# Block sums of two seven-product projections made by accumulating transfers, and two attention heads placed between the first two products

## The chip, the cores and the metric

The kernel runs on one core of one Trainium2 chip. The metric is the time of one execution on the device in microseconds (us). A core has five engines, each with an instruction queue of its own: PE (matrix multiplication), ACT (activation functions, copies, casts), DVE (elementwise work), POOL, and SP, which here only issues transfers. POOL issues transfers too. Engines wait for one another through semaphores; in the rows of instructions further down, "waits DVE_49" is such a wait, DMAHW names the semaphores of transfers issued by SP, and DMASW those of transfers issued by POOL.

## The reference

The reference is one layer of a hybrid decoder trunk on 512 tokens of width 1024, in fp32, with a memory of 256 tokens:

```python
h = rmsnorm(x, norm_mix_g)
proj = h @ w_in                       # 1024 x 8192: three branches and their gates
conv_out = short_conv_mixer(...)      # causal depthwise convolution, 512 channels
sb_out = stick_breaking_attention(...)# 8 heads x 64
ret_out = retention(...)              # 4 heads x 128
up = einsum('bsnw,nwd->bsnd', branches, w_branch)
gates = sigmoid(gate_logits + b_gate)
merged = sum(gates * up, axis=2)
x = x + merged @ w_o                  # 1024 x 1024: the first output projection
h = rmsnorm(x, norm_xa_g)
mem_n = rmsnorm(mem, norm_mem_g)
q, k, v = h @ w_xq, *split(mem_n @ w_xkv)
o = softmax(q k^T / 16) v             # 4 heads x 256
x = x + o @ w_xo                      # 1024 x 1024: the second output projection
h = rmsnorm(x, norm_mlp_g)
x = x + square(relu(h @ w_up)) @ w_down
return rmsnorm(x, final_g)
```

## The kernel before

*Arithmetic.* Every fp32 operand of a matrix product is split into a high part, a cast to fp32r made on ACT, and a low part, the difference from it, made on DVE. A product is three matrix multiplications: high by high, high by low and low by high. For weights the split is `parts_of` (L111 the cast, L112 the subtraction); for the token side it is `split` (L260, L261).

*The weight stream.* Weights arrive in blocks of 128 x 1024 (512 KB), issued by SP (L214) into six buffers named `w_raw`. Their parts go into ten buffers named `w_part`. A list of items, `plan`, written out in program order, says which parts each item takes; `Stream.pump` makes the parts two steps ahead of the item that needs them. A scheduler then sets the order of the instructions on each engine; each engine works through its own list strictly in that order.

*Seven products instead of eight.* The projections by `w_o`, `w_xo` and `w_down` use a seven-product form of the 2 x 2 block product. On the weight side this is `Wide`: an entry takes eight blocks, named b11, b12, b22 and b21 with j = 0 and 1 each, and makes 14 parts of it in the order

```python
P1,0 P5,0 P1,1 P5,1 P6,0 P6,1 P3,0 P3,1 P2,0 P2,1 P7,0 P7,1 P4,0 P4,1
```

Each part is used by 12 matrix multiplications of 128x512 (L399). j halves the contraction: j = 0 takes the first 512 rows of the weight. P1 takes b11 as it is, P3 b22, P2 b21; for P5, P6, P4 the block b11 is overwritten, step by step, by a sum or difference with another block, and b12 once for P7 (`step`: L127 a subtraction, L130 an addition, on DVE). So in all there are eight block sums per projection of `w_o` and `w_xo`, each an instruction over 128 x 1024 elements.

On the token side `Pairs.make` forms the matching mixes (`pr_v`, `mg` or `xo_u`) on DVE and splits them into `pr` and `pr_b`. `items_w` lists the products: each is accumulated in PSUM and added to x (L405), at the place that the table `TO` gives.

*The two places.* `proj_norm` writes out a projection with the following RMSNorm, and is called for `w_o` and for `w_xo`.

Around `w_o`: the branch outputs are being multiplied by `w_branch`, gated by sigmoids (`gt`, L885) and merged into `mg` (L840, L841), from which the mixes are made; the gate's own products (`seven`, L329, with copies into `sv_s` and `sv_u`) run between the first products of `w_o`. `reload_x` loads x again from DRAM (`load_x`, L99, issued by POOL), since x is the residual. `mem_begin` then loads the gains `g_mem` (L93) and two tiles of the memory (`m_sb`, L928), also from POOL; ACT's norm of the memory reads them (L465).

Around `w_xo`: the products of `w_xv` end (`xv_h`, `xv_l`). Then each head h of four has its scores (`xa_scores`), softmax, the transposes of its probabilities (`xa_transpose`: `xpp` by PE, `xpT` the parts), and its output (`xa_out`: 12 matrix multiplications of `xpT` with `xv`, four copies into `xo_s` and `xo_u` at L1073 and L1074, and the pairs). Heads 0 and 1 feed the products with j = 0, heads 2 and 3 those with j = 1. Before, the order at the end is written out as

```python
    item(lambda: xa_out(2))
    item(lambda: xa_out(3))
    ...
    proj_norm(w_xo, "xo", g_mlp, lambda p: None, first_up)
```

so that both of the last heads stand ahead of every product of `w_xo`.

Of the kernel before, what the change touches and what calls it, by code (L numbers as in the profile page):

```python
# [15 lines left out]
P = 128  # L16
# [22 lines left out]
def trunk_kernel(ctx: ExitStack, tc: tile.TileContext, x, mem, par, rot, dqd, kdec, g_mix, g_xa, g_mem, g_mlp,  # L39
# [56 lines left out]
    def load_x():  # L96
        xs = [unit("x", (P, D), F32) for _ in range(NT)]
        for t in range(NT):
            pool.dma_start(out=xs[t], in_=x[t * P:(t + 1) * P, :])  # L99
        return xs  # L100
# [28 lines left out]
    def plus(out, a, b):  # L129
        dve.tensor_tensor(out=out, in0=a, in1=b, op=ALU.add)  # L130

# [42 lines left out]
    class Wide:  # L174
# [3 lines left out]
        def __init__(self, t, c):  # L178
            self.loads = [(t, c + i) for i in range(8)]
            at = dict(P1=0, P5=1, P6=4, P3=4, P2=6, P7=6, P4=6)  # L180
            self.need = [at[p] + (2 * j if at[p] < 4 else j) + 1 for p, j in ORDER]
            self.steps = [lambda raw, p=p, j=j: self.step(raw, p, j) for p, j in ORDER]
            self.parts = []

        def step(self, raw, p, j):
            b11, b12, b22, b21 = (raw[i] if i < len(raw) else None for i in (2 * j, 2 * j + 1, 4 + j, 6 + j))
            if p == "P5":
                minus(b11, b12, b11)
            elif p == "P6":
                plus(b11, b22, b11)  # L190
                plus(b12, b12, b22)
            elif p == "P4":
                minus(b11, b21, b11)
            return parts_of(dict(P3=b22, P2=b21, P7=b12).get(p, b11))

# [153 lines left out]
    class Pairs:  # L349
# [7 lines left out]
        def make(self, e, s, u):  # L357
# [14 lines left out]
            minus(u[:, 1, :], u[:, 1, :], u[:, 0, :])  # L372
# [4 lines left out]
    TO = dict(P1=(0, 0), P2=(0, 0), P3=(0, 1), P4=(2, 0), P5=(2, 1), P6=(0, 1), P7=(2, 1))  # L377

    def items_w(src, c, pairs, after=lambda p: None):
# [4 lines left out]
        def part(p, js, n):  # L384
            bank = dict(P2="p2", P5="p3", P3="p3").get(p, "p1")

            def fn(ws):
# [14 lines left out]
                def add(i):  # L402
                    t, h = TO[p]
                    dst = S["x"][t + i][:, h * 512:(h + 1) * 512]
                    dve.tensor_tensor(out=dst, in0=acc[bank, i], in1=dst, op=ALU.add)  # L405
# [7 lines left out]
            item(fn, (Wide, src, c, n, n + len(js)))  # L413
# [549 lines left out]
    def proj_norm(src, name, g, beside, after):  # L963
# [20 lines left out]
        items_w(src, 0, lambda k: S[name, k // 2].w[k % 2], ends)  # L984
# [106 lines left out]
    item(lambda: xa_out(2))  # L1091
    item(lambda: xa_out(3))
# [43 lines left out]
    proj_norm(w_xo, "xo", g_mlp, lambda p: None, first_up)  # L1136
# [152 lines left out]
```

## Time and profile before

| | us |
|---|---|
| median of 3 runs | 1032.84 |
| lowest, highest | 1031.75, 1033.41 |
| the profiled execution, its own time | 1034.26 |
| span of the profiled execution | 1032.5 |
| PE busy | 1000.0 (97%) |
| DVE busy | 732.8 (71%) |
| ACT busy | 529.3 (51%) |
| POOL busy | 69.2 (7%) |

The mean granted TensorE clock of the profiled execution is 0.992 of full speed. The span reaches from the first to the last instruction on the core; the time of an execution is a little longer. In rows of the timeline the columns are start, duration, engine, line, operation, output and input tiles with their shapes, a count, and in brackets the idle time of that engine ahead of the row and what ended it. In rows of groups the two numbers behind the bar are the busy time and the mean duration in ns, and behind the second bar the idle time ahead. A time between the start of a row and the start of the next one on the same engine is what it costs there; the durations of neighbouring rows overlap a little. In the table of windows each engine has its busy time, then the granted clock, the share of DMA engines that were busy, and GB/s. In rows of transfers the last number is the median time from issue to landing.

### The profile page before, as it was taken

To read this page: it belongs to the slowest core of one execution; us is meant where nothing else is said; L and a number is where in the kernel's file an instruction comes from. 1 tells how busy PE (TensorE), PEld (TensorE's weight loads), DVE (VectorE), ACT (ScalarE), POOL (GpSimd) and SP (SyncE) were. 2 spreads that over 40 slices of the span, in tenths; PEclk is the share of its full clock that TensorE was granted. 3 is DMA by queue.
4 is the path that set the end of the run, shared out by engine and by line. 5 is a ranking of instruction groups with operands and counts; after the bars stand their busy time and mean duration, and the time that the engine had idled before them with its cause. 6 is when DMAs were issued, how large, how long until landed. Compare 5 with 4: busy or idle time off the path is not lost.

```text
span 1032.5 us, 13357 instructions
## 1 busy us (share of the span) xinstructions
PE 1000.0 (97%) x5060; PEld 846.0 (82%) x5060; DVE 732.8 (71%) x1092; ACT 529.3 (51%) x935; POOL 69.2 (7%) x128
## 2 busy tenths in 40 slices
PE   5999999999999999998999998999999999999996
PEld 4788888888888889997798886779888888888885
DVE  5567767866453797789796469694785695686785
ACT  5475566766532245465474346464553653553543
POOL 1111103321010000001000000000000000000000
PEclk9999999999999999999899999999999999999999
DMA  8322232213222212325445210152125115215212
GB/s 326 103 82 85 83 123 99 83 42 110 74 80 84 82 46 98 103 88 186 153 174 185 92 62 21 60 189 79 41 102 177 49 62 175 91 41 184 82 42 82
DMA packets 29873, 106.28 MB, mean 103 GB/s; under 512 B 3568, under 2 KB 3568, under 8 KB 29808
## 3 DMA queue, kind: packets, MB, share of 16 engines
q1 hardware_dynamic: 27216, 98.05, 27.4%
q0 software_dynamic: 1440, 5.24, 1.4%
q10 hardware_dynamic: 1152, 2.12, 0.6%
q8 instruction: 40, 0.66, 0.3%
q14 instruction: 25, 0.20, 0.1%
HBM read 103.31 MB, written 2.10 MB: 102 GB/s over the span
## 4 chain that ended last, share of the span: by engine, by line
PE 92%; DVE 4%; DMA 1%; ACT 1%; issue 1%; SPq 0%; POOL 0%; DVEq 0%; POOLq 0%; ACTq 0%
PE p L399 21%; PE mm L272 20%; PE mm L273 20%; PE mm L271 20%; PE p L329 5%; DVE w_part L112 1%; PE o L657 1%; PE at L496 1%; PE aT L623 1%; DMA w_raw<-in_w_in_dram 1%; PE z L599 1%; PE z L600 0%; DVE w_raw L130 0%; PE ro L804 0%; PE sc L778 0%
## 5 line engine op out<-in xcount | busy, mean ns | idle before, releaser
L112 DVE TENSOR_TENSOR w_part<-w_raw,w_part 128x1024 fp32r<-128x1024 f32 (+1 forms) x228 | 274.7, 1207 | 155.1 <-ACT w_part L111 141.3
L111 ACT CAST w_part<-w_raw 128x1024 fp32r<-128x1024 f32 (+1 forms) x228 | 236.6, 1040 | 284.4 <-PE mm L272 146.0
L272 PE MATMUL mm<-hT_l,w_part 128*128 128x512 f32 (+1 forms) x704 | 268.0, 381 | 1.7 <-DVE hT_l L261 1.7
L273 PE MATMUL mm<-hT_h,w_part 128*128 128x512 f32 (+1 forms) x704 | 267.9, 381 | 0.0
L271 PE MATMUL mm<-hT_h,w_part 128*128 128x512 f32 (+1 forms) x704 | 267.3, 382 | 0.0
L399 PE MATMUL p<-w_part,pr 128*128 128x512 f32 x864 | 206.2, 394 | 3.8 <-ACT pr L260 2.7
L399 PEld LDWEIGHTS p<-w_part,pr 128*128 128x128 f32 x864 | 162.7, 190 | 40.3 <-ACT pr L260 3.1
L272 PEld LDWEIGHTS mm<-hT_l,w_part 128*128 128x128 f32 x704 | 132.5, 188 | 25.8 <-DVE hT_l L261 1.9
L273 PEld LDWEIGHTS mm<-hT_h,w_part 128*128 128x128 f32 x704 | 132.5, 188 | 24.8
L271 PEld LDWEIGHTS mm<-hT_h,w_part 128*128 128x128 f32 x704 | 131.8, 188 | 23.7
L405 DVE TENSOR_TENSOR x<-p,x 128x512 f32<-128x512 f32 x84 | 56.8, 684 | 20.5 <-PE p L399 20.4
L399 PE MATMUL p<-w_part,pr_b 128*128 128x512 f32 x144 | 37.1, 411 | 2.4 <-ACT w_part L111 2.4
L127 DVE TENSOR_TENSOR w_raw<-w_raw 128x1024 f32<-128x1024 f32 (+1 forms) x36 | 37.5, 1042 | 0.8 <-DMA w_raw<-in_w_xo_dram 0.3
L611 DVE TENSOR_TENSOR_SCAN sb_suf<-ones,sb_e 128x128 f32<-128x128 f32 (+3 forms) x32 | 29.6, 926 | 11.3 <-POOL sb_e L590 9.6
L130 DVE TENSOR_TENSOR w_raw<-w_raw 128x1024 f32<-128x1024 f32 (+1 forms) x36 | 37.4, 1039 | 0.1
L329 PE MATMUL p<-mix_h,w_part 128*128 128x256 f32 x192 | 37.0, 283 | 0.0
L399 PEld LDWEIGHTS p<-w_part,pr_b 128*128 128x128 f32 x144 | 28.5, 199 | 9.5 <-ACT w_part L111 2.8
L329 PEld LDWEIGHTS p<-mix_h,w_part 128*128 128x128 f32 x192 | 30.9, 191 | 0.2
L465 ACT ACTIVATE xn<-x 128x512 f32<-128x512 f32 x32 | 20.0, 628 | 19.4 <-DVE x L405 16.2
L614 ACT ACTIVATE sb_suf<-sb_suf 128x128 f32<-128x128 f32 (+3 forms) x32 | 15.1, 471 | 27.7 <-DVE sb_suf L613 27.7
L329 PE MATMUL p<-hT_h,w_part 128*128 128x256 f32 x144 | 28.6, 283 | 0.4 <-ACT w_part L111 0.4
L329 PE MATMUL p<-mix_l,w_part 128*128 128x256 f32 x96 | 27.1, 283 | 0.0
(225 smaller groups left out, 1466.4 us busy)
## 6 DMA issues: line engine op xcount, KB each, us to landing
w_raw<-in_w_in_dram SPq DMA_DIRECT2D x52, 512.0 KB, 3.5
w_raw<-in_w_up_dram SPq DMA_DIRECT2D x32, 512.0 KB, 3.5
w_raw<-in_w_down_dram SPq DMA_DIRECT2D x32, 512.0 KB, 3.5
w_raw<-in_w_br_dram SPq DMA_DIRECT2D x12, 512.0 KB, 3.4
w_raw<-in_w_gate_dram SPq DMA_DIRECT2D x12, 512.0 KB, 3.5
w_raw<-in_w_o_dram SPq DMA_DIRECT2D x8, 512.0 KB, 4.0
w_raw<-in_w_xk_dram SPq DMA_DIRECT2D x8, 512.0 KB, 3.5
w_raw<-in_w_xv_dram SPq DMA_DIRECT2D x8, 512.0 KB, 3.5
```

What stands on the lines that cost most here:

```text
L111: act.copy(out=wh, in_=src)
L112: dve.tensor_tensor(out=wl, in0=src, in1=wh.bitcast(F32), op=ALU.subtract)
L127: dve.tensor_tensor(out=out, in0=a, in1=b, op=ALU.subtract)
L130: dve.tensor_tensor(out=out, in0=a, in1=b, op=ALU.add)
L271: te.matmul(ps, lh, rh, start=first, stop=False)
L272: te.matmul(ps, lh, rl, start=False, stop=False)
L273: te.matmul(ps, ll, rh, start=False, stop=last)
L329: te.matmul(ps[:, :256], x[:, k, :], y, start=first and k == 0 and i == 0, stop=k == 3 and i == 2, skip_group_check=True)
L399: te.matmul(acc[bank, i], x, y, start=p in ("P1", "P5", "P2") and j + k + m == 0, stop=j == 1 and k == 1 and m == 2, skip_group_check=True)
L405: dve.tensor_tensor(out=dst, in0=acc[bank, i], in1=dst, op=ALU.add)
L465: act.activation(out=dst[:, cs], in_=src[:, cs], func=AF.Square, accum_out=ss[:, i:i + 1])
L611: dve.tensor_tensor_scan(out=suf[:, :s][:, ::-1], data0=ones[:, :s], data1=e1[:, :s][:, ::-1], initial=0.0, op0=ALU.mult, op1=ALU.add)
```

## The change

- `Summed`, a new kind of `Wide`, is used by both calls of `proj_norm`. The eight block sums of a projection are no longer instructions of DVE. They are transfers that POOL issues (L212 in the new file) with the option to add: they read the other block from DRAM once more and add it to what stands in the `w_raw` buffer. In the step of P1: b11 += b12 and b12 += b22; in that of P5: b11 += b22; in that of P6: b11 += b21. Each is issued after the parts of that step have been made, which read the buffer.
- Since an accumulating transfer only adds, the signs are changed throughout: `Wide.step` adds where it subtracted, `Pairs.make` forms its mixes with the opposite sign (`neg`, a scalar_tensor_tensor in place of a tensor_tensor), and `TO` says for each product whether it is added to x or subtracted from it. `Wide` itself stays in use for `w_down`, with its sums on DVE.
- `load_x` is issued by SP instead of POOL.
- `last_heads` puts heads 2 and 3 between the first product (P1,0) and the second (P5,0) of `w_xo`.

```diff
     def load_x():
...
-            pool.dma_start(out=xs[t], in_=x[t * P:(t + 1) * P, :])
+            nc.sync.dma_start(out=xs[t], in_=x[t * P:(t + 1) * P, :])
...
     class Wide:
...
             if p == "P5":
-                minus(b11, b12, b11)
+                plus(b11, b11, b12)
             elif p == "P6":
-                plus(b11, b22, b11)
+                plus(b11, b11, b22)
                 plus(b12, b12, b22)
             elif p == "P4":
-                minus(b11, b21, b11)
+                plus(b11, b11, b21)
             return parts_of(dict(P3=b22, P2=b21, P7=b12).get(p, b11))
+
+    class Summed(Wide):
+        def __init__(self, t, c):
+            super().__init__(t, c)
+            self.need = [n + (n in (1, 3)) for n in self.need]
+
+        def step(self, raw, p, j):
+            b11, b12, b22, b21 = (raw[i] if i < len(raw) else None for i in (2 * j, 2 * j + 1, 4 + j, 6 + j))
+
+            def acc(dst, i):
+                pool.dma_start(out=dst, in_=self.t[self.c + i], accum_op=ALU.add)
+
+            parts = parts_of(dict(P3=b22, P2=b21, P7=b12).get(p, b11))
+            if p == "P1":
+                acc(b11, 2 * j + 1)
+                acc(b12, 4 + j)
+            elif p in ("P5", "P6"):
+                acc(b11, 4 + j if p == "P5" else 6 + j)
+            return parts
...
+            def neg(out, a, b):
+                dve.scalar_tensor_tensor(out=out, in0=a, scalar=-1.0, in1=b, op0=ALU.mult, op1=ALU.subtract)
...
-            minus(v, u[:, 0:1, :].broadcast_to([P, 2, 256]), s)
+            minus(v, s, u[:, 0:1, :].broadcast_to([P, 2, 256]))
             put(("A11", "A22"), s)
-            minus(u[:, 0, :], s[:, 0, :], v[:, 1, :])
+            neg(u[:, 0, :], s[:, 0, :], v[:, 1, :])
...
-            minus(u[:, 1, :], u[:, 1, :], u[:, 0, :])
+            neg(u[:, 1, :], u[:, 1, :], u[:, 0, :])
...
-    TO = dict(P1=(0, 0), P2=(0, 0), P3=(0, 1), P4=(2, 0), P5=(2, 1), P6=(0, 1), P7=(2, 1))
+    TO = dict(P1=(0, 0, plus), P2=(0, 0, plus), P3=(0, 1, minus), P4=(2, 0, plus), P5=(2, 1, minus), P6=(0, 1, minus),
+              P7=(2, 1, minus))
...
-    def proj_norm(src, name, g, beside, after):
+    def proj_norm(src, name, g, beside, after, first=lambda its: None):
...
-        items_w(src, 0, lambda k: S[name, k // 2].w[k % 2], ends)
+        its = capture(lambda: items_w(src, 0, lambda k: S[name, k // 2].w[k % 2], ends, Summed))
+        first(its)
+        plan.extend(its)
...
-    item(lambda: xa_out(2))
-    item(lambda: xa_out(3))
+    def last_heads(its):
+        plan.append(its.pop(0))
+        item(lambda: xa_out(2))
+        item(lambda: xa_out(3))
+        plan.append(its.pop(0))
...
-    proj_norm(w_xo, "xo", g_mlp, lambda p: None, first_up)
+    proj_norm(w_xo, "xo", g_mlp, lambda p: None, first_up, last_heads)
```

Where the instructions stand is shown at three places. The number behind a tile's name tells its buffers apart. The line numbers of the new file are higher from L130 on (L260 is L286, L885 is L915, L1073 is L1105, L399 is L429, L1054 is L1086, L928 is L958).

POOL at `w_o`. The raws are 4051 (b11, j = 0), 4053 (b12, j = 0), 4059 (b11, j = 1) and 4227 (b12, j = 1). Before:

```order
L99 DMA x_4392<-in_x_dram 128x1024 [waits PE_49]
L99 DMA x_4393<-in_x_dram 128x1024 [waits PE_49]
L99 DMA x_4394<-in_x_dram 128x1024 [waits DVE_49,PE_49]
L99 DMA x_4395<-in_x_dram 128x1024 [waits DVE_49,PE_49]
L93 DMA g_bc_4408<-in_g_mem_dram 128x1024 [waits DMAHW6_49,DVE_49,PE_49]
L928 DMA m_sb_4410<-in_mem_dram 128x1024 [waits PE_49,Activation_49]
L928 DMA m_sb_4411<-in_mem_dram 128x1024 [waits DVE_49,PE_49]
```

And in the new order:

```order
L212 DMA w_raw_4053<-in_w_o_dram 128x1024 [waits DMAHW4_49,DMAHW2_49,DMAHW6_49,DMAHW0_49,DVE_49]
L212 DMA w_raw_4227<-in_w_o_dram 128x1024 [waits DMAHW4_49,DMAHW2_49,DMAHW5_49,DMAHW0_49,DVE_49]
L212 DMA w_raw_4051<-in_w_o_dram 128x1024 [waits DMAHW5_49,DMAHW3_49,DMAHW7_49,DMAHW1_49,DVE_49]
L212 DMA w_raw_4051<-in_w_o_dram 128x1024 [waits DMASW2_49,DVE_49]
L212 DMA w_raw_4059<-in_w_o_dram 128x1024 [waits DMAHW3_49,DMAHW7_49,DMAHW1_49,DVE_49]
L212 DMA w_raw_4059<-in_w_o_dram 128x1024 [waits DMASW4_49,DVE_49]
L212 DMA w_raw_4051<-in_w_o_dram 128x1024 [waits DMASW3_49,DVE_49]
L212 DMA w_raw_4059<-in_w_o_dram 128x1024 [waits DMASW5_49,DVE_49]
L93 DMA g_bc_4410<-in_g_mem_dram 128x1024 [waits DMASW0_49]
L958 DMA m_sb_4412<-in_mem_dram 128x1024 [waits DMASW1_49,PE_49]
L958 DMA m_sb_4413<-in_mem_dram 128x1024 [waits PE_49]
```

The loads of x have left POOL; on SP they now stand behind the sixth load of `w_o` and ahead of its last two. The eight sums stand ahead of the loads for the memory.

ACT at `w_o`. The casts into `w_part` are, in this order, those of P1,1 (from 4059), P5,1 (4059), P6,0 (4051) and P6,1 (4059); the last one before, from 4229, is P3,0's. Before:

```order
L111 CAST w_part_4414<-w_raw_4059 128x1024 [waits DMAHW7_49,PE_49]
L339 COPY sv_u_4250<-p1_4246 128x256 [waits PE_49]
L885 ACTIVATE gt_4341<-sv_s_4249,prm_82 128x256 [waits DVE_49]
L260 CAST pr_4214<-mg_2857 128x512 [waits DVE_49]
L885 ACTIVATE gt_4359<-sv_u_4250,prm_82 128x256 [waits DVE_49]
L111 CAST w_part_4433<-w_raw_4059 128x1024 [waits DVE_49,PE_49]
L885 ACTIVATE gt_4359<-sv_s_4249,prm_82 128x256 [waits DVE_49]
L111 CAST w_part_4453<-w_raw_4051 128x1024 [waits PE_49]
L885 ACTIVATE gt_4341<-p1_4246,prm_82 128x256 [waits PE_49]
L111 CAST w_part_4473<-w_raw_4059 128x1024 [waits DVE_49]
L260 CAST pr_b_4201<-mg_2990 128x256 [waits DVE_49]
L111 CAST w_part_4515<-w_raw_4229 128x1024 [waits DMAHW1_49,PE_49]
```

And in the new order:

```order
L111 CAST w_part_4416<-w_raw_4059 128x1024 [waits DMAHW7_49,PE_49]
L365 COPY sv_u_4252<-p1_4248 128x256 [waits PE_49]
L915 ACTIVATE gt_4343<-sv_s_4251,prm_82 128x256
L915 ACTIVATE gt_4361<-sv_u_4252,prm_82 128x256 [waits DVE_49]
L915 ACTIVATE gt_4361<-sv_s_4251,prm_82 128x256 [waits DVE_49]
L111 CAST w_part_4436<-w_raw_4059 128x1024 [waits DMASW4_49,PE_49]
L111 CAST w_part_4455<-w_raw_4051 128x1024 [waits DMASW3_49,PE_49]
L286 CAST pr_b_4201<-mg_2990 128x256 [waits DVE_49]
L915 ACTIVATE gt_4343<-p1_4248,prm_82 128x256 [waits PE_49]
L286 CAST pr_4381<-mg_2990 128x512 [waits DVE_49]
L111 CAST w_part_4474<-w_raw_4059 128x1024 [waits DMASW5_49]
L286 CAST pr_4385<-pr_v_4379 128x512 [waits DVE_49]
```

The casts of P5,1, P6,0 and P6,1 wait for a transfer (DMASW) where they followed a sum of DVE, and the sigmoid of p1 and the casts of `pr` now stand behind them.

PE at `w_xo`, from the last head's multiplications on in the old order, and from the transposes of the last two heads on in the new one. p is the accumulator of P1 and P5. Before:

```order
L273 MATMUL mm<-xpT,xv_l 128x512 x2
L1054 MATMUL xpp<-ident,x_p 128x128 x2
L399 MATMUL p_5942<-w_part,pr 128x512 x6
L399 MATMUL p_5943<-w_part,pr 128x512 x6
L399 MATMUL p_5961<-w_part,pr 128x512 x5
L1054 MATMUL xpp<-ident,x_p 128x128 x2
L399 MATMUL p_5961<-w_part,pr 128x512
```

And in the new order:

```order
L1086 MATMUL xpp<-ident,x_p 128x128 x6
L429 MATMUL p_5875<-w_part,pr 128x512 x6
L429 MATMUL p_5876<-w_part,pr 128x512 x3
L1086 MATMUL xpp<-ident,x_p 128x128 x2
L429 MATMUL p_5876<-w_part,pr 128x512 x3
L297 MATMUL mm<-xpT,xv_h 128x512
```

The 12 multiplications of P1,0 now run ahead of those of head 2, and those of P5,0 follow head 3. On ACT, in the same place, `xv_h` stands behind the casts of P5,1 and P6,0, which wait for the transfers:

```order
L111 CAST w_part_5960<-w_raw_5656 128x1024 [waits DMASW0_49,PE_49]
L286 CAST xv_h_4406<-mm_5727 128x512 [waits PE_49]
L111 CAST w_part_5979<-w_raw_5493 128x1024 [waits DMASW7_49,PE_49]
L286 CAST xv_h_4407<-mm_5734 128x512 [waits PE_49]
L286 CAST xpT_5817<-xpp_5812 128x2x256 [waits PE_49]
L286 CAST xpT_5817<-xpp_5841 128x2x256 [waits PE_49]
L111 CAST w_part_5998<-w_raw_5656 128x1024 [waits DMASW1_49,PE_49]
L1105 COPY xo_s_5890<-mm_5892 128x256 [waits PE_49]
```

Before, each of the two `xv_h` casts there stood one place ahead of its weight cast:

```order
L260 CAST xpT_5717<-xpp_5764 128x2x256 [waits PE_49]
L260 CAST xv_h_4404<-mm_5727 128x512 [waits PE_49]
L111 CAST w_part_5957<-w_raw_5656 128x1024 [waits DVE_49]
L260 CAST xv_h_4405<-mm_5734 128x512 [waits PE_49]
L111 CAST w_part_5977<-w_raw_5493 128x1024
L260 CAST xpT_5817<-xpp_5812 128x2x256 [waits PE_49]
```

More of the change, by code (lines that the diff above doesn't have):

```diff
@@ L178, in __init__ @@
         def __init__(self, t, c):
+            self.t, self.c = t, c
             self.loads = [(t, c + i) for i in range(8)]
@@ L371, in make, with items_w @@
             split(hi, lo, u[:, 1, :])
-            minus(u[:, 1, :], u[:, 1, :], u[:, 0, :])
+            neg(u[:, 1, :], u[:, 1, :], u[:, 0, :])
             put(("S2", "S4"), u)
     LEFT = dict(P1="A11", P2="A12", P3="S4", P4="A22", P5="S1", P6="S2", P7="S3")
-    TO = dict(P1=(0, 0), P2=(0, 0), P3=(0, 1), P4=(2, 0), P5=(2, 1), P6=(0, 1), P7=(2, 1))
-    def items_w(src, c, pairs, after=lambda p: None):
+    TO = dict(P1=(0, 0, plus), P2=(0, 0, plus), P3=(0, 1, minus), P4=(2, 0, plus), P5=(2, 1, minus), P6=(0, 1, minus),
+              P7=(2, 1, minus))
+    def items_w(src, c, pairs, after=lambda p: None, kind=Wide):
         acc = {}
@@ L402, in add @@
                 def add(i):
-                    t, h = TO[p]
+                    t, h, op = TO[p]
                     dst = S["x"][t + i][:, h * 512:(h + 1) * 512]
-                    dve.tensor_tensor(out=dst, in0=acc[bank, i], in1=dst, op=ALU.add)
+                    op(dst, dst, acc[bank, i])
                 rows = p in ("P7", "P4")
@@ L412, in fn @@
                         add(i)
-            item(fn, (Wide, src, c, n, n + len(js)))
+            item(fn, (kind, src, c, n, n + len(js)))
         for n, (p, j) in enumerate(ORDER):
```

## The prediction

> **What bounds the kernel now.** I read the busy shares and the chain of the page first, then a table of the two stages in question by window, then the timelines around their gaps.
>
> ```profile
> PE 1000.0 (97%) x5060; PEld 846.0 (82%) x5060; DVE 732.8 (71%) x1092; ACT 529.3 (51%) x935; POOL 69.2 (7%) x128
> ...
> PE 92%; DVE 4%; DMA 1%; ACT 1%; issue 1%; SPq 0%; POOL 0%; DVEq 0%; POOLq 0%; ACTq 0%
> ```
>
> PE carries the chain, so time can only come from the places where PE starves. Two of them lie where the change works:
>
> ```profile
> core 0: us, PE busy (x) PEld busy (x) DVE busy (x) ACT busy (x) POOL busy (x), PEclk, DMA share, GB/s
> 475.00:480.00 5.00, 5.00 (x34) 4.50 (x33) 5.00 (x8) 3.43 (x5) 0.72 (x2) 1.00 0.96 356
> 480.00:485.00 5.00, 4.01 (x21) 2.89 (x19) 5.00 (x7) 1.27 (x2) 0.00 (x0) 1.00 0.08 30
> 485.00:490.00 5.00, 2.85 (x10) 1.72 (x10) 5.00 (x8) 3.70 (x6) 0.00 (x0) 1.00 0.09 17
> 490.00:495.00 5.00, 2.38 (x5) 1.23 (x6) 5.00 (x7) 1.66 (x2) 0.00 (x0) 0.81 0.54 193
> 495.00:500.00 5.00, 5.00 (x13) 3.89 (x13) 2.55 (x5) 1.04 (x1) 0.00 (x0) 0.51 0.33 108
> 640.00:645.00 5.00, 1.39 (x5) 0.48 (x3) 5.00 (x9) 2.99 (x11) 0.00 (x0) 0.82 0.00 0
> 645.00:650.00 5.00, 4.13 (x11) 3.39 (x12) 3.38 (x8) 1.43 (x3) 0.00 (x0) 0.50 0.00 0
> ```
>
> In both, DVE is full (5.00 of 5.00) while PE idles, and the granted clock then falls to about 0.5. The rows below price the work and mark its ends.
>
> ```profile
> L127 DVE TENSOR_TENSOR w_raw<-w_raw 128x1024 f32<-128x1024 f32 x24 | 29.3, 1219 | 0.6 <-DMA w_raw<-in_w_xo_dram 0.3
> L112 DVE TENSOR_TENSOR w_part<-w_raw,w_part 128x1024 fp32r<-128x1024 f32 (+1 forms) x228 | 274.7, 1207 | 155.1 <-ACT w_part L111 141.3
> L111 ACT CAST w_part<-w_raw 128x1024 fp32r<-128x1024 f32 (+1 forms) x228 | 236.6, 1040 | 284.4 <-PE mm L272 146.0
> 787.25 2.72 PE p L399 x12
> ...
> 464.17 1.21 DVE L112 TENSOR_TENSOR w_part<-w_raw,w_part 128x1024 fp32r<-128x1024 f32 x1
> 469.88 1.05 ACT L111 CAST w_part<-w_raw 128x1024 fp32r<-128x1024 f32 x1 [0.36 <-PE mm L272]
> 473.98 0.37 ACT L339 COPY sv_u<-p 128x256 f32<-128x256 f32 x1 [0.61 <-PE p L329]
> 475.69 0.28 PE L329 MATMUL p<-mix_h,w_part 128*128 128x256 f32 x1
> 480.83 0.39 PE L399 MATMUL p<-w_part,pr 128*128 128x512 f32 x1
> 481.03 0.47 ACT L885 ACTIVATE gt<-p,prm 128x256 f32<-128x256 f32 x1 [1.04 <-PE p L329]
> 486.43 0.69 DVE L127 TENSOR_TENSOR pr_v<-mg 128x512 f32<-128x512 f32 x1
> 487.07 2.90 PE L399 MATMUL p<-w_part,pr 128*128 128x512 f32 x10 [2.72 <-ACT pr L260]
> 493.31 5.90 PE L399 MATMUL p<-w_part,pr_b 128*128 128x512 f32 x12 [2.40 <-ACT w_part L111]
> 505.82 0.62 ACT L465 ACTIVATE xn<-m_sb 128x512 f32<-128x512 f32 x1
> ...
> 621.82 1.22 DVE L112 TENSOR_TENSOR w_part<-w_raw,w_part 128x1024 fp32r<-128x1024 f32 x1 [3.60 <-ACT w_part L111]
> 637.75 0.39 PE L271 MATMUL mm<-xpT,xv_h 128*128 128x512 f32 x1
> 645.87 0.66 PE L1054 MATMUL xpp<-ident,x_p 128*128 128x128 f32 x2 [3.75 <-DVE x_p L1046]
> 662.20 1.10 PE L399 MATMUL p<-w_part,pr 128*128 128x512 f32 x3 [0.42 <-DVE pr L261]
> ```
>
> A part is 12 matmuls, 2.72 us at full clock, 0.227 each. In w_o, 24 matmuls of P1 and P5 stand between 480.83 and 493.31: 5.45 us of work in 12.48, so 7.0 lost, and the half clock behind (12 in about 5.7) costs 2.8 more: at most 9.8 to win. In w_xo, between 637.75 and 662.65 stand 48 + 24 matmuls and 8 transposes, about 17.05 us of work in 24.9: at most 7.85.
>
> **The change, part by part.** *Removed:* eight block sums on DVE per projection at 1.22 us, 9.8 us each, out of the stretches where DVE was full. *Negation* by scalar_tensor_tensor, `op` and the plus form of Wide are the same count of DVE instructions of the same size; DVE is off the path there: nothing. *x on SP:* four issues behind six w_o loads. In the order the seventh w_o load is next; before, it was issued at 488.61, x at 468.29, so 20 us cover it:
>
> ```profile
> 468.29 2.56 POOL L99 DMA_DIRECT2D x<-in_x_dram  x4 [116.68 <-PE mm L273]
> 488.61 3.34 SPq L214 DMA_DIRECT2D w_raw<-in_w_o_dram  x2
> ```
>
> *mem on POOL:* g_mem and m_sb now queue behind the eighth sum, which waits for P6,1's low part (about 492.3 below); issued near 494, landed by 500, read at 505.82 before. Hidden, with 5 us over; if the sums slip by more, ACT's norm of mem slips next.
>
> POOL spends about half a microsecond on issuing each transfer, and it has nothing else in either stage but these sums and mem:
>
> ```profile
> 474.64 0.54 POOL L928 DMA_DIRECT2D m_sb<-in_mem_dram  x1
> ```
>
> *Added:* sixteen accumulating loads. They read 524 KB each once more, 4.2 MB per projection, 11.8 us of all DMA engines at the 356 GB/s of the 475 row. In w_xo the share is 0.00 and they have room; in w_o the 475 row is at 0.96 and only the rows from 480 to 490 (0.08, 0.09) are free. Their landing time L, from the release of the sum to the moment at which the next cast may start, decides all. No row shows one. The nearest are plain 512 KB loads from POOL, quiet (3.9) and in traffic (5.2, 5.7):
>
> ```profile
> g_bc<-in_g_mlp_dram POOLq DMA_DIRECT2D x1, 512.0 KB, 3.9
> x<-in_x_dram POOLq DMA_DIRECT2D x4, 512.0 KB, 5.2
> m_sb<-in_mem_dram POOLq DMA_DIRECT2D x2, 512.0 KB, 5.7
> ```
>
> Lower end 3.9. An add must also fetch its target, one more pass of 524 KB, 1.47 us at the 356 GB/s of the 475 row: 5.4. Upper end two whole loads, 7.8. I take 5.4, nearest to the quiet row, and add about 1 where other loads overlap.
>
> *w_o with L = 5.4.* A sum may start only when the low part of the undisturbed block has been made, since it writes over the block; the cast of the sum then waits for the landing. ACT and DVE take everything in order, so what stands behind that cast waits too. These are the rows of the work that stands there:
>
> ```profile
> 484.20 1.04 ACT L111 CAST w_part<-w_raw 128x1024 fp32r<-128x1024 f32 x1 [2.70 <-DVE w_raw L130]
> 486.41 0.61 ACT L260 CAST pr<-mg 128x512 fp32r<-128x512 f32 x1
> 488.50 0.68 DVE L261 TENSOR_TENSOR pr<-mg,pr 128x512 fp32r<-128x512 f32 x1
> ```
>
> The first is P6,1's cast, which waited for its DVE sum before. The sums of b12 are wanted only by P7, much later, but they share the queue with those of b11. P1,0's low part ends at 465.4; the first sum, beside x, lands at 472.2, 2.3 later than P5,0's cast was. Behind that cast on ACT, P1,1's cast and the sv_u copy move to 474.9, still ahead of PE's 475.69: no loss. P5,0's low part ends at 474.45, P1,1's at 476.3. Sum 1 of j = 1 is issued at 476.4, overlaps sum 2 of j = 0, and lands at 482.3. P5,1's cast takes ACT till then, and the sigmoid stands behind P5,1, P6,0 and pr_b: 484.7 instead of 481.03. But DVE has no sums in front of the rest: pr_v starts at 487.4, only 0.95 later than 486.43. P5,1's low part ends at 484.55, its sum lands at 490.0; P6,1's cast waits for it, and pr_v's cast behind that ends at 491.65, its low part at 493.3. The last two matmuls of P5,1 end at 493.75; the next part began at 493.31. So +0.4: the sums' waits replace DVE's. Each further us of L costs 2 here, two sums being in series.
>
> *w_xo.* Here nothing of the merge is in the way, and the heads stand behind the casts:
>
> ```profile
> 638.02 0.59 ACT L260 CAST xv_h<-mm 128x512 fp32r<-128x512 f32 x1
> 640.65 0.68 DVE L261 TENSOR_TENSOR xv_l<-mm,xv_h 128x512 fp32r<-128x512 f32 x1
> 641.93 0.37 ACT L1073 COPY xo_s<-mm 128x256 f32<-128x256 f32 x1
> ```
>
> P1,0's low part ends at 623.0; the sum lands at 628.4, when DMA is idle; P5,0's cast follows (to 629.4), low parts at 630.5 and 631.8. Sum 1 of j = 1, overlapped, lands at 638.0, just as PE ends w_xv (637.75, plus 0.3). P5,1's cast, xv_h, P6,0's cast, xv_h end at 641.2, their low parts at 642.8. PE meanwhile runs transposes and P1,0 (12 matmuls, now ahead of the heads) to 641.5, and needs the first xv low part at 642.4: no stall over 0.4. P5,1's low part ends at 640.2, sum 2 lands at 645.6 and holds ACT till 646.7, with the copies of head 2 behind it. Four copies at 0.37, the mixes and a cast of 0.61 with its low part of 0.68 make the first pairs ready at 648.9. PE wants them at 649.7: 641.5 plus 24 head matmuls (5.45) plus P5,0 (2.72). Head 3's pairs stall it 0.3 and 0.7. The 24 matmuls of P1,1 and P5,1 (5.45) and these stalls end at 656.0 instead of 662.65: -6.6.
>
> What makes this stage so much better than w_o is that P1,0 and P5,0 now lie on either side of the heads: PE has 2.72 us of work where it waited for xv, and 2.72 where it waited for the pairs. That part of the gain does not need the sums to be fast; what needs it is ACT's order, in which xv_h stands behind P5,1's cast.
>
> Sum: +0.4 - 6.6 = -6.2; 1034.26 becomes 1028.1 for a run like the profiled one. That run was 1.42 above the median, 1032.84, so 1026.6.
>
> At L = 3.9, w_o gains 4.0 and w_xo 7.0: about 1022 (less with the half clock gone). At 6.5, w_o loses 2.6 and w_xo keeps 2.8: even. At 8, w_o loses 5.6, and w_xo, with PE waiting 5 us for xv, loses 3.5: 1042. So each us of L costs 2 in w_o and up to 4 in w_xo, where both xv and the pairs come late.
>
> Clock: the rows halve it from 493 after gaps of 2.72 and 2.40, so I keep the half clock in w_o, whose gaps become 1.9, 1.2, 1.0 and 2.3. The Trainium skill (TensorE: Matmul & The Clock Gate, Part 1) has the clock fall only after an idle window of about 3.4 us. By that rule no gap here would halve it, and the sum would be 2.8 lower, 1023.8; the 495 row contradicts it, so the row decides.
>
> The Trainium skill (Collectives: The Full Stack, The bandwidth ceiling) says that the add in a DMA costs no time but its second read does, halving the rate; with the fit of DMA: Bandwidth & Descriptors (2.0 us plus bytes at 436 GB/s) I estimate 4.4 for L, and a sum of about -9. No run so far shows it, and the fit gives 3.2 for the plain load that the trace has at 3.9.
>
> **Rivals.**
> - *The accumulate is slow* (L over 6.5, up to 8): ACT, in order, holds at P5,1's and P6,1's casts, and xv_h, sigmoid and pr casts stand behind. For it: ACT's order, four sums in a chain per projection, traffic rows at 5.7. Against it: DMA is at 0 GB/s in w_xo. Slower from L = 6.5 on, 1042 at 8.
> - *It lands like a plain load* (L about 4): for it the 3.9 row; against it the second read. 1022.
> - *Waits trade places* (L of 6.2 to 6.5): the gain of w_xo goes into w_o. 1032 to 1034.
>
> **Numbers.** Forecast 0.43 (L 4.5 to 6.2), plain 0.15, even 0.10, slow 0.32. No change is within 0.2%, 2.1 us, about what a measurement of this kernel can tell: faster 0.58, same 0.10, slower 0.32. The range 1022 to 1042 leaves out the tips below 4.0 and above 8, about 2 in 10; the forecast alone spans 1023 to 1031.
>
> **What would show it.** Right: the issues of w_raw from POOL landing in 5 to 6 us; DVE busy well below 5.00 in the two stages; no stall over 1 us from 637 to 662, at full clock; PE's first part after P5 near 493.7 in w_o; no wait of ACT for m_sb. Wrong: casts on ACT waiting over 6 us for w_o and w_xo loads; a PE gap before the head matmuls with xv as its releaser; landing times above 6.5, or DMA shares in w_xo near 1 that show the sums queueing behind each other.

## The result and the profile after

The changed kernel is slower: 1038.27 us (median; 1037.2 to 1039.56) against 1032.30 for the kernel before on the same chip, a ratio of 1.0057 (95% interval 1.0041 to 1.0072), or +5.9 us. The forecast was 1026.6 in a range of 1022 to 1042, so the time lies inside the range and on the other side of the time before. One execution of `e16_late_x_sp` further down ran at a granted clock of 0.559 and took 1684.1 us; it is left out.

The page of the changed kernel: PE is as busy as before, and DVE has lost 17 us of work. The chain of work that ended last could be followed back over 38% of the span only; PE has 34 of that.

```profile
span 1036.5 us, 13401 instructions
PE 1001.1 (97%) x5060; PEld 846.2 (82%) x5060; DVE 716.1 (69%) x1076; ACT 528.5 (51%) x935; POOL 81.2 (8%) x140
...
PE 34%; DVE 2%; issue 1%; DMA 1%; ACT 0%; DVEq 0%; POOLq 0%; POOL 0%; ACTq 0%
```

The table by windows of the `w_o` stage, in answer to the one shown of before (PE, weight loads, DVE, ACT, POOL, granted clock, DMA share, GB/s):

```profile
475.00:480.00 5.00, 2.32 (x18) 2.02 (x17) 3.29 (x4) 3.30 (x6) 1.06 (x2) 1.00 0.75 277
480.00:485.00 5.00, 3.93 (x24) 3.31 (x22) 1.81 (x3) 0.91 (x2) 0.70 (x1) 1.00 1.03 188
485.00:490.00 5.00, 1.94 (x4) 1.24 (x5) 2.42 (x3) 2.67 (x4) 0.87 (x1) 0.65 0.05 8
490.00:495.00 5.00, 5.00 (x16) 3.68 (x14) 3.24 (x6) 1.11 (x2) 0.88 (x1) 0.66 0.86 159
495.00:500.00 5.00, 2.06 (x7) 0.97 (x6) 4.42 (x6) 3.49 (x5) 2.49 (x4) 1.00 0.53 89
500.00:505.00 5.00, 3.73 (x9) 2.96 (x10) 3.01 (x6) 0.00 (x0) 0.00 (x0) 0.52 0.97 276
```

DVE, full before, is idle for a third to two thirds of most of these rows, and PE starves more than before. The timeline of the same place says for what: the casts of the sums (L111), the stalls of PE behind them, and the load of b21 on SP.

```profile
464.15 1.21 DVE L112 TENSOR_TENSOR w_part<-w_raw,w_part 128x1024 fp32r<-128x1024 f32 x1
464.96 1.78 POOL L212 DMA_DIRECT2D w_raw<-in_w_o_dram  x2 [13.99 <-DMA w_raw<-in_w_o_dram]
475.49 1.04 ACT L111 CAST w_part<-w_raw 128x1024 fp32r<-128x1024 f32 x1 [6.17 <-DMA w_raw<-in_w_o_dram]
478.05 0.73 PE L429 MATMUL p<-w_part,pr 128*128 128x512 f32 x2 [2.68 <-ACT w_part L111]
478.31 1.22 DVE L112 TENSOR_TENSOR w_part<-w_raw,w_part 128x1024 fp32r<-128x1024 f32 x1
486.50 1.99 ACT L111 CAST w_part<-w_raw 128x1024 fp32r<-128x1024 f32 x2 [5.29 <-DMA w_raw<-in_w_o_dram]
487.60 0.79 PE L429 MATMUL p<-w_part,pr 128*128 128x512 f32 x1 [3.67 <-ACT w_part L111]
494.51 1.05 ACT L111 CAST w_part<-w_raw 128x1024 fp32r<-128x1024 f32 x1 [2.26 <-DMA w_raw<-in_w_o_dram]
498.91 1.46 SPq L240 DMA_DIRECT2D w_raw<-in_w_o_dram  x2
501.27 10.93 PE L429 MATMUL p<-w_part,pr 128*128 128x512 f32 x35 [2.73 <-DVE x L130]
```

From the end of a low part (465.36, 479.53, and 488.8 for the third) to the cast of the sum takes 10.1, 7.0 and 5.7 us. In `w_xo` the same three intervals are 5.7, 7.5 and 5.9 us (630.01 to 635.72, 639.67 to 647.16, 649.47 to 655.34):

```profile
635.72 1.05 ACT L111 CAST w_part<-w_raw 128x1024 fp32r<-128x1024 f32 x1 [1.40 <-DMA w_raw<-in_w_xo_dram]
647.16 1.05 ACT L111 CAST w_part<-w_raw 128x1024 fp32r<-128x1024 f32 x1 [4.26 <-DMA w_raw<-in_w_xo_dram]
655.34 1.05 ACT L111 CAST w_part<-w_raw 128x1024 fp32r<-128x1024 f32 x1 [4.24 <-DMA w_raw<-in_w_xo_dram]
```

Three rows of PE's timeline split the difference by stage: the first product of `w_xq`, the last of `w_xv`, and the first of `w_up`. Those of before, then of the changed kernel:

```profile
563.56 0.39 PE L271 MATMUL mm<-hT_h,w_part 128*128 128x512 f32 x1
637.52 0.39 PE L273 MATMUL mm<-w_part,mT_l 128*128 128x512 f32 x1
692.88 0.72 PE L271 MATMUL mm<-hT_h,w_part 128*128 128x256 f32 x4
```

```profile
570.52 0.39 PE L297 MATMUL mm<-hT_h,w_part 128*128 128x512 f32 x1
644.49 0.39 PE L299 MATMUL mm<-w_part,mT_l 128*128 128x512 f32 x1
696.63 0.71 PE L297 MATMUL mm<-hT_h,w_part 128*128 128x256 f32 x4
```

Up to `w_xq` the changed kernel is 6.96 us late; from there to the end of `w_xv` both take 74.0; from there to `w_up` it takes 52.14 instead of 55.36, 3.2 less. So `w_o` lost 7 and `w_xo` gave back 3.2. Two windows of `w_xo`, of which the prediction shows the rows before (PE 1.39 and 4.13 us busy, clock 0.82 and 0.50):

```profile
640.00:645.00 5.00, 5.00 (x25) 4.11 (x24) 2.57 (x8) 1.02 (x4) 0.94 (x1) 1.00 1.05 185
645.00:650.00 5.00, 4.72 (x23) 3.29 (x21) 1.76 (x3) 2.84 (x4) 0.24 (x1) 1.00 0.10 19
```

PE no longer starves there, at full clock. The DMA share of 1.05, with two sums in flight, is one of the prediction's signs of being wrong, and so is the wait of 6.17 us for the first sum of `w_o`.

### The profile page after: what moved, and what is told of

Its sections match the earlier page's. It is cut to its first block, busy times and chain, and to the rows that moved or that the text cites. A ratio compares the mean times of both kernels' runs of the same rounds, so it can differ in the third digit from the quotient of the medians.

```text
span 1036.5 us, 13401 instructions
## 1 busy us (share of the span) xinstructions
PE 1001.1 (97%) x5060; PEld 846.2 (82%) x5060; DVE 716.1 (69%) x1076; ACT 528.5 (51%) x935; POOL 81.2 (8%) x140
## 5 line engine op out<-in xcount | busy, mean ns | idle before, releaser
L111 ACT CAST w_part<-w_raw 128x1024 fp32r<-128x1024 f32 (+1 forms) x228 | 236.1, 1040 | 302.5 <-PE mm L298 144.1
L429 PE MATMUL p<-w_part,pr 128*128 128x512 f32 x864 | 209.4, 398 | 13.1 <-ACT w_part L111 6.4
L429 PEld LDWEIGHTS p<-w_part,pr 128*128 128x128 f32 x864 | 164.4, 192 | 51.9 <-ACT w_part L111 6.8
L130 DVE TENSOR_TENSOR w_raw<-w_raw 128x1024 f32<-128x1024 f32 (+1 forms) x44 | 47.2, 1073 | 0.3
L127 DVE TENSOR_TENSOR x<-x,p 128x512 f32<-128x512 f32 x48 | 32.5, 680 | 11.6 <-PE p L429 11.6
L429 PE MATMUL p<-w_part,pr_b 128*128 128x512 f32 x144 | 33.8, 389 | 0.0
L130 DVE TENSOR_TENSOR x<-x,p 128x512 f32<-128x512 f32 x36 | 24.1, 681 | 11.6 <-PE p L429 11.4
L429 PEld LDWEIGHTS p<-w_part,pr_b 128*128 128x128 f32 x144 | 27.0, 188 | 5.6
```

The lines of the kernel that those rows point to most:

```text
L111: act.copy(out=wh, in_=src)
L127: dve.tensor_tensor(out=out, in0=a, in1=b, op=ALU.subtract)
L429: te.matmul(acc[bank, i], x, y, start=p in ("P1", "P5", "P2") and j + k + m == 0, stop=j == 1 and k == 1 and m == 2, skip_group_check=True)
```

## The experiments

Each ratio is to the kernel before on the same chip, with its 95% interval. "Marks" are the start of `w_xq` (before 563.56) and the stretch from `w_xv` to `w_up` (before 55.36), read in the profiled execution as above. The start of `w_xq` varies between executions: where `w_o` was as before and x on POOL, it stood at 561.2 to 562.6 in the experiments. Differences between runs are taken from the ratios.

### Which stage, which part

`e1_xo_only`: sums by transfer in `w_xo` alone, heads moved.

```diff
-    proj_norm(w_o, "mp", g_xa, mem_beside, kv_proj)
+    proj_norm(w_o, "mp", g_xa, mem_beside, kv_proj, kind=Wide)
...
-            nc.sync.dma_start(out=xs[t], ...)
+            pool.dma_start(out=xs[t], ...)
```

> Sums by transfer and the moved heads in w_xo alone; w_o keeps its sums on DVE, x and the memory are loaded by POOL as before. Theory A (the whole loss of the change lies in w_o, where the sums meet the loads of b22 and x, and w_xo gains by itself): in the changed kernel the end of w_xv came 6.97 us later and the end of the first two products of w_xo only 3.45 us later, so this stage gained 3.5; here the kernel should be 3.5 us faster, about 1029, its sums landing in 5.7 alone and 7.5 in pairs. Theory B (w_xo gained only because everything ahead of it was late, so that heads and loads had more time): less than 1.5 us faster.

Measured 1030.04, ratio 0.9968 (0.9957 to 0.9979), -3.3 us; marks 562.04 and 51.75. Theory A holds.

`e2_o_only`: sums by transfer in `w_o` alone.

```diff
-    proj_norm(w_xo, "xo", g_mlp, lambda p: None, first_up, last_heads)
+    item(lambda: xa_out(2))
+    item(lambda: xa_out(3))
+    proj_norm(w_xo, "xo", g_mlp, lambda p: None, first_up, kind=Wide)
```

> Sums by transfer in w_o alone (x on SP); w_xo as before, with its sums on DVE and both heads ahead. Theory A: w_o costs 7.0 and nothing of it is given back, so about 1039.5, that is slower than the changed kernel by 1 us or more. Theory B (part of the lateness is swallowed by the stages between): 1035 to 1037. The first sum into b11 should again land in about 10 us, the paired ones in 7, the lone one in 5.7.

Measured 1042.20, ratio 1.0088 (1.0072 to 1.0103), +9.1; marks 571.73 and 55.61. Theory A holds, with more lost than it said. The two stages add: 9.1 - 3.3 = 5.8, and the change measured 5.9.

`e3_heads_only` (all sums on DVE, only `last_heads`) and `e4_xo_sums` (as `e1_xo_only`, but without `last_heads`):

> All sums on DVE, x on POOL; only the order is changed: heads 2 and 3 between the first two products of w_xo. Theory A (the 3.5 us that w_xo gained come from both parts, DVE being full there): the 2.72 us of P1,0 cover part of the wait for xv, DVE stays full, and the gain is 1 to 2 us. Rival: the order alone gives all of it, 3 us or more, and the transfers give nothing in w_xo either. Other rival: no gain, since DVE carries the same work.

> Sums by transfer in w_xo, both heads ahead of all products as before; w_o as before. Theory A: the cast of P5,1 waits for a paired sum (7.5 us), xv_h stands behind it on ACT, and PE has no P1,0 to run in that time: the gain of the freed DVE is eaten, 0 to 3 us slower than before. Rival (freed DVE time is what counts): 2 to 4 us faster.

`e3_heads_only` measured 1033.38, ratio 1.0002 (0.9993 to 1.0011): nothing. `e4_xo_sums` measured 1028.65, ratio 0.9962 (0.9950 to 0.9975), the same gain as with the heads moved; the expected loss was wrong. The instructions of `e1_xo_only` and `e4_xo_sums` stand in the same order on every engine, row for row: the scheduler put P1,0 ahead of the heads by itself as soon as DVE's sums were gone, and moving the items in the list does nothing (`e3_heads_only` has the order of before on PE, ACT, POOL and SP). So the gain of 3.2 in `w_xo` comes with the sums: from the time they free on DVE and from the order that the scheduler then makes, two causes that no run parts. `e3_heads_only` also has all the new signs, so these are free within 1 us.

`e9_x_sp`: sums and heads as before, new signs, x on SP.

> All sums on DVE and the heads as before; the signs are the new ones, and x is reloaded by SP. Both theories: the signs and the queue of x are free, within 0.5 us of the time before. If x on SP matters (it now stands ahead of the last two loads of w_o), the loads of b21 come later than 488.6 and the kernel is slower by more than 1 us.

Measured 1034.87, ratio 1.0014 (1.0005 to 1.0023). x on SP costs about 1.4 us (0.5 to 2.4 by the interval). Its profiled execution (marks 563.40 and 54.71) shows no place for that, and which wait it is stays open.

### What makes the sums late

`e7_copy`: the same sixteen transfers overwrite instead of adding, so the sums are left out.

```diff
-                pool.dma_start(out=dst, in_=self.t[self.c + i], accum_op=ALU.add)
+                pool.dma_start(out=dst, in_=self.t[self.c + i])
```

> The changed kernel with the same sixteen transfers that overwrite instead of adding, so the sums are left out and everything else stays. If the addition itself is what makes the landing slow (a second pass over the target, 1.5 us estimated from 524 KB at 356 GB/s), the lone transfers land in about 4 instead of 5.7, those in pairs in 5 instead of 7 to 7.5, and the kernel is 5 to 8 us faster than the changed one, at or below the time before. If traffic and the order decide, landings fall by less than 1 us and the kernel gains less than 3.

Measured 1027.50, ratio 0.9940 (0.9926 to 0.9953); marks 562.35 and 47.56. The addition costs about 12 us of the whole, more than expected. The windows from 467 to 472, when x, b22's loads and two sums are in flight, in the changed kernel and then in this one:

```profile
467.00:472.00 5.00, 5.00 (x24) 4.14 (x23) 3.67 (x8) 1.99 (x5) 0.00 (x0) 1.00 1.03 202
467.00:472.00 5.00, 5.00 (x24) 4.14 (x23) 3.62 (x8) 2.53 (x6) 0.00 (x0) 1.00 0.99 384
```

The DMA engines are full in both, but while they add they move 202 GB/s instead of 384. The Trainium skill (Collectives: The Full Stack, The bandwidth ceiling) says of a reduce-scatter that its add needs two source reads on the same ring, and that it so gets about half the rate of a copy; these rows, with two sums among plain loads, agree. The pages of the two profiles have, for the queue that POOL issues to, its packets, MB and the time its packets took as a share of 16 engines' span, changed and then copying:

```profile
q0 software_dynamic: 3168, 11.54, 5.4%
q0 software_dynamic: 3168, 11.54, 3.3%
```

Packets and bytes are the same. 5.4% of 1036.5 us and 3.3% of 1025.1 us differ by 22 us, so by an estimate from these rows each of the sixteen sums holds all DMA engines about 1.4 us longer than a copy. The transfers of `w_o` and `w_xo` in the list of DMA issues (median us to landing), changed and then copying:

```profile
w_raw<-in_w_o_dram POOLq DMA_DIRECT2D x8, 512.0 KB, 6.2
w_raw<-in_w_xo_dram POOLq DMA_DIRECT2D x8, 512.0 KB, 5.7
```

```profile
w_raw<-in_w_o_dram POOLq DMA_DIRECT2D x8, 512.0 KB, 4.7
w_raw<-in_w_xo_dram POOLq DMA_DIRECT2D x8, 512.0 KB, 3.6
```

`e5_no_x`: x is not reloaded, the first addition into each part of x copies; the residual of `w_o` is left out.

> The changed kernel without the reload of x: the first addition into each part of x copies instead, so the residual of w_o is left out. Theory A (traffic): the first sum into b11 of w_o no longer shares the DMA engines with 2 MB of x and lands in 6.5 to 7 us instead of 10.1; the stall of 2.68 us behind it goes, and 3 to 4 us of the loss in w_o with it: about 1034.5. Theory C (the chain of sums on ACT's order costs by itself, whatever the traffic): less than 1 us faster than the changed kernel.

Measured 1037.85, ratio 1.0038 (1.0026 to 1.0051), at most 2 us better than the changed kernel; marks 569.81 and 51.57. The cast of the first sum stood at 475.37 instead of 475.49. That x is what makes it late falls. In the changed kernel the queue of the sums took 99.3% of the engines' time from 467.9 to 471 and that of SP 4.9%, so x hardly moved while two sums were in flight.

`e6_b12_dve`: the sums into b12 back on DVE, at the step of P6.

```diff
-                acc(b12, 4 + j)
             elif p in ("P5", "P6"):
                 acc(b11, 4 + j if p == "P5" else 6 + j)
+            if p == "P6":
+                plus(b12, b12, b22)
```

> The changed kernel with the two sums into b12 of each projection back on DVE, at the step of P6: four transfers fewer per two projections, and no sum shares its flight with one into b12. Theory A (traffic): only the second of the b12 sums of w_o is issued right ahead of the first b11 sum, so that one lands 1 to 1.5 us earlier (8.5 to 9 instead of 10.1): 1 to 2 us faster than the changed kernel. Theory C: DVE has 2.4 us more to do in each stage and the kernel is the same or slower.

Measured 1034.52, ratio 1.0016 (1.0007 to 1.0025): 4 us better than the changed kernel; marks 566.60 and 51.78. The first sum's cast stands at 472.68. So the b12 sums are in the way, more than expected.

`e10_b12_late` issues the b12 sums at the step of P6 and keeps them transfers:

```diff
             if p == "P1":
                 acc(b11, 2 * j + 1)
-                acc(b12, 4 + j)
...
+            elif p == "P6":
+                acc(b12, 4 + j)
```

> The changed kernel with the sums into b12 issued at the step of P6 instead of P1, behind the sums into b11 that casts wait for; still all sixteen are transfers. Theory D (a sum moves at about half the rate of a plain load, so each one in flight delays the others by about 2.6 us; the early b12 sums are in the way of b11's): the first sum into b11 of w_o lands near 472.7 as it did with b12 on DVE, and the kernel gains 3.5 to 5 us on the changed one, to 1033.5 to 1034.5. If the gain with b12 on DVE had another cause (the order that the scheduler made of it), less than 1.5 us.

Measured 1039.08, ratio 1.0058 (1.0045 to 1.0070). This tested nothing: each engine's order is that of the changed kernel, row for row, so the scheduler seems to issue a transfer as soon as its block is there. `e15_b12_forced` holds them back by a dependence:

```diff
+            elif p == "P6":
+                lo = parts[1].bitcast(F32)
+                dve.scalar_tensor_tensor(out=b12[:, :1], in0=lo[:, :1], scalar=0.0, in1=b12[:, :1],
+                                         op0=ALU.mult, op1=ALU.add)
+                acc(b12, 4 + j)
```

> The changed kernel with the sums into b12 held back behind the low part of P6 by an element-wise instruction on one column of b12 that also reads that low part (four small instructions on DVE); all sixteen sums stay transfers. This time the order on POOL has the b11 sums first. Theory D (sums in flight halve the rate for one another): the first sum into b11 of w_o lands near 472.7 instead of 475.5, w_xq starts 3 to 4.5 us earlier than in the changed kernel, and the time is 1034 to 1035. If the gain with b12 on DVE was the order, or DVE's, less than 1.5 us are gained.

Measured 1034.72, ratio 1.0016 (1.0007 to 1.0026); marks 567.25 and 51.89. The cast of the first sum, in its timeline:

```profile
473.17 2.00 ACT L111 CAST w_part<-w_raw 128x1024 fp32r<-128x1024 f32 x2 [3.87 <-DMA w_raw<-in_w_o_dram]
```

It comes 2.3 us earlier than in the changed kernel, with all sixteen sums still transfers, and 4.2 us are gained, the same as with b12 on DVE. So early b12 sums, which nobody waits for, cost 4.2 of the 9.1 us in `w_o`. The other 4.9 is a remainder: it holds the b11 sums, which casts wait for, and x on SP (about 1.4 by `e9_x_sp`), and no run parts them further.

### Only the sums that nobody waits for

`Late` leaves the b11 sums of P5 and P6 on DVE, and makes those into b12 (for P7) and of b21 (for P4) transfers.

```diff
+            if p == "P5":
+                plus(b11, b11, b12)
+            elif p == "P6":
+                plus(b11, b11, b22)
             parts = parts_of(...)
+            if p == "P6":
+                acc(b12, 4 + j)
+                acc(b11, 6 + j)
```

`e11_xo_b12_late` (all sums of `w_xo`, b12's at the step of P6), `e12_late` (all sums of `w_xo`, `Late` in `w_o`), `e13_late_both` (`Late` in both), `e14_xo_late` (`Late` in `w_xo` alone), `e16_late_x_sp` (`Late` in both, x on SP); heads as before in all, and x on POOL in the first four. `e11_xo_b12_late` came out with the order of `e4_xo_sums` on every engine, for the reason seen at `e10_b12_late`; the two ratios are of one kernel, and agree.

> Sums by transfer in w_xo alone, heads as before, with the sums into b12 issued at the step of P6. Theory D: in w_xo the b12 sums are issued long before (607 us and earlier) and meet nothing, so nothing changes against the run with sums in w_xo and the heads as before: 1028.6 within 1 us. Rival: the four late sums meet the loads of b21 and w_up and cost 1 to 3 us.

> Sums by transfer in w_xo as in the run with the heads as before, and in w_o only the four sums that are wanted late (into b12 for P7, of b21 for P4), issued at the step of P6; those of P5 and P6 into b11 stay on DVE, and x on POOL. Theory E (DVE is what w_o lacks, and only sums without a waiting cast may leave it): two of the four sums of 1.22 us leave the crowded stretch, 1.5 to 2.5 us faster than w_xo alone, so 1026 to 1027. Rival from theory D: the late sums are issued at about 487, when the loads of b21 are (488.6), and slow them by 2 to 4 us; P2 waits for b21, and the kernel is 1 to 3 us slower than with w_xo alone.

> In both projections only the four late sums are transfers; all sums into b11 for P5 and P6 stay on DVE, heads and x as before. If the gain in w_xo comes from DVE time in the crowded stretch (637 to 650), where two of the eight sums of b12 and three or four of b11 ran, about half of it remains: 2 us faster than before, less or more what w_o does in the run with late sums there. If what w_xo needs is the b11 sums off DVE, nothing remains: within 0.7 us of before.

> Only the four late sums of w_xo are transfers (into b12 for P7, of b21 for P4); the sums into b11 for P5 and P6 stay on DVE, w_o is as before, x on POOL. Theory F (a transfer is worth it only where no cast waits for it): the stretch from the end of w_xv to the first product of w_up, 55.4 us before, 52.1 changed and 48.7 with late sums in both projections, is 48.7 here, and w_o costs nothing: 6 to 7.5 us faster than before, 1025.5 to 1027. Rival (the gain of the run with late sums in both came half from w_o): 4 us faster or less.

> The late sums alone as transfers in both projections, and x reloaded by SP, so that x does not stand behind sums on POOL (there it was issued at 485.6 and landed in 9.5 to 10). If that was what kept late sums from helping in w_o: faster than with late sums in w_xo alone, by 1 to 2.5 us, 1024 to 1025. If the loads of b21 and the sums share the DMA engines to the harm of P2 (it waited 3.0 for a cast that waited for b21): no better than with w_xo alone, 1026 to 1028.

| | median us | ratio (interval) | `w_xq` | `w_xv` to `w_up` |
|---|---|---|---|---|
| `e11_xo_b12_late` | 1030.18 | 0.9969 (0.9958 to 0.9981) | 562.53 | 51.80 |
| `e12_late` | 1032.21 | 0.9994 (0.9986 to 1.0003) | 563.77 | 52.57 |
| `e13_late_both` | 1029.13 | 0.9958 (0.9946 to 0.9970) | 563.49 | 48.65 |
| `e14_xo_late` | 1027.05 | 0.9935 (0.9923 to 0.9947) | 562.55 | 48.69 |
| `e16_late_x_sp` | 1030.47 | 0.9968 (0.9955 to 0.9981) | 565.01 | 48.63 |

`e14_xo_late` is 6.7 us faster than before and the best of all: theory F holds. Four sums off DVE that no cast waits for are worth 6.7 us in `w_xo`, all eight only 3.2 to 3.9. `e13_late_both` gained 4.3, twice what was expected. PE's waits from 600 to 700 in that kernel, of which the first (norm) was there before too:

```profile
PE mm L316 <- DVE hT_l L305: 1.7, 1, 1.7
PE at L544 <- ACT hT_h L304: 0.4, 1, 0.4
PE mm L316 <- DVE xpT L305: 0.3, 1, 0.3
PE xpp L1104 <- DVE x_p L1096: 0.2, 1, 0.2
```

The wait of 3.7 for `x_p` that stood there before is gone, though DVE is still full or nearly so (4.53 and 5.00 of 5.00 from 645 to 655).

In `w_o` late sums cost 2.4 to 3.4 us (`e13_late_both` and `e16_late_x_sp` against `e14_xo_late`, `e12_late` against `e4_xo_sums`). The scheduler puts x behind them, and then x, the memory and the sums meet the loads of b21. DMA issues from 484 to 493 in `e16_late_x_sp`, where the load of `w_o` took 3.4 before:

```profile
x<-in_x_dram SPq DMA_DIRECT2D x4, 512.0 KB, 11.7
w_raw<-in_w_o_dram SPq DMA_DIRECT2D x2, 512.0 KB, 10.5
```

And PE's timeline there:

```profile
494.98 5.31 PE L447 MATMUL p<-w_part,pr_b 128*128 128x512 f32 x12 [4.69 <-ACT w_part L111]
```

P2 then waits 4.69 us for b21, 2.40 before. That is the rival of `e12_late`, and it held with x on either queue.

## Why the prediction was wrong

- **What bounds it: right.** PE is 97% busy before and after, and the whole difference lies in the two stages named.
- **L in quiet: nearly right.** 5.4 was taken; a lone sum took 5.7 to 5.9 from release to cast, 5.3 to 5.5 from issue to landing. The second pass, put at 1.47 us, took about 1.4. The 4.4 that the prediction worked out from the Trainium skill was too low, as was the 3.2 for the plain load.
- **L beside other transfers: the step that failed.** "About 1" was added for overlap. With a sum at about half the rate, every other sum in flight costs more (about 2.3 us for the one b12 sum ahead of the first b11 sum, by `e15_b12_forced`): 10.1 against the 6.8 worked out for the first sum of `w_o`, 7.0 against 5.9 for its pair, 7.5 against 6.2 for the pair in `w_xo`. `e7_copy` and `e15_b12_forced` showed both halves of that: the rate, and the early b12 sums in the queue. The sentence that the b12 sums "share the queue" stood in the text, but carried no term. Behind the first late cast PE waited 2.68 us where the prediction had "no loss".
- **w_o +0.4: measured +7.0 in the profiled executions, +9.1 alone.** PE's first part after P5 began at 501.27, where the prediction had 493.75. Behind the late casts, ACT's order also pushed P3's casts, so that the loads of b21 went from 488.61 to 498.91, and PE took P6 ahead of P2 and waited 2.73 for an addition into x. The prediction kept the next part at its place. Even with landings like plain ones (`e7_copy`), `w_o` gained nothing or 1 us, not the 4.0 forecast for such landings (2.6 by the prediction's own 2 us for each us of L): the first cast stood at 471.46, 6.1 after its release, beside x and b22.
- **w_xo -6.6: measured -3.2.** The sign and the mechanism held: no stall of PE from the end of `w_xv` to 666 is over 0.92 us, and with landings like plain ones (`e7_copy`) the stage took 7.8 less than before, near the 7.0 forecast. The pair landed 2.7 us after the last product of `w_xv` instead of 0.5, and the next sum 10.9 after it instead of 8.1, with the copies of head 2 behind its cast.
- **The heads: wrong in the cause.** "That part of the gain does not need the sums to be fast" took the list of items for the cause of the order. The order shown came with the sums, not with the list; what it is worth by itself no run shows.
- **x on SP at nothing: wrong by about 1.4.** The signs at nothing: right.
- **mem hidden with 5 us over: hidden, with less over.** Issued at 498.20 and 498.74 instead of 474.64 and 475.56, landing 10.5 and 12.5 us later, read at 513.37. No row shows ACT waiting for it, and PE's timeline shows no wait between 501.27 and the first product of `w_xq`.
- **Clock: the price was right, the count was not.** The prediction kept one stretch at half clock in `w_o`. There were two of 6.83 us (486.53 to 493.36 and 500.18 to 507.01; before, 493.06 to 499.88), and PE was busy in them for 11.0 us instead of 6.5. Half of the busy time is the loss, so that is an estimated 2.3 of the 7.0 us lost. In `w_xo` the stretch of before (643.24 to 650.07, PE busy 4.2 us) is gone, an estimated 2.1 of the 3.2 gained. These are figures of the two profiled executions. The rule of the Trainium skill (TensorE: Matmul & The Clock Gate, Part 1) would not have halved the clock after a gap of 2.73 us; the row from 500 to 505 above, 0.52, differs from it.
- **The rival "slow accumulate"** named this outcome and its place on ACT, with the cause in L itself; the cause was the company of other transfers. The range holds the measured time through this rival, not through the forecast.

## What to carry to other kernels

An accumulating transfer takes an elementwise sum off a full engine. Here it was worth it where nothing waited for its landing and few loads stood beside it: four such sums gave 6.7 us in `w_xo`, four more that casts waited for took 3 back, and in `w_o`, where loads stood beside them, four cost 2.4 to 3.4. Count every one in flight at half the rate, the ones that nobody waits for too, since they delay the others. And where a scheduler sets the order, compare the orders of the engines before testing a reordering: two edits to the list left every engine's order as it was, and only a dependence moved the transfers.

## What was not expected of the hardware

- Full DMA engines moved 202 GB/s with sums among the transfers and 384 without (467 to 472, share 1.03 and 0.99). Plain loads beside the sums slow down with them: x, issued by SP, took 8.3 us against 6.2 in `e7_copy` (5.2 before, issued by POOL).
- POOL needs 0.88 us for issuing an accumulating transfer; with the same transfer overwriting it is 0.54. A row of the changed kernel's timeline, and one of `e7_copy`:

```profile
489.10 0.87 POOL L212 DMA_DIRECT2D w_raw<-in_w_o_dram  x1 [8.40 <-DVE w_part L112]
```

```profile
474.07 0.54 POOL L212 DMA_DIRECT2D w_raw<-in_w_o_dram  x1 [7.92 <-DVE w_part L112]
```

- A gap of 2.68 us of PE, up to 478.05, left the granted clock at 1.00, while one of 2.73, up to 501.27, halved it. The windows of the changed kernel around the two:

```profile
478.00:482.00 4.00, 3.95 (x23) 3.53 (x24) 3.01 (x6) 1.70 (x4) 1.75 (x2) 1.00 0.67 119
502.00:504.00 2.00, 2.00 (x7) 1.52 (x5) 1.01 (x2) 0.00 (x0) 0.00 (x0) 0.50 0.87 254
```

In the profile before, the gap of 2.72 us up to 487.07 left the row from 485 to 490 at 1.00, and the clock fell, at 493.06, within the one of 2.40 up to 493.31. All four stretches at half clock in the two kernels' stages lasted 6.83 us. So the length of one gap alone does not set it; what does was not tried.
